# Moving the mLSTM query eviction from VectorE to ScalarE by taking the norm's scale out of it

## The chip, the cores and the metric

The kernel runs on one core of one Trainium2 chip. The metric is the device time of one execution in microseconds (us), the median of several runs. A core has five engines that run side by side, each with its own in-order list of instructions: TensorE (PE, matmuls; its weight loads are shown apart as PEld), VectorE (DVE), ScalarE (ACT), GpSimd (POOL) and SyncE (SP, which here only issues DMAs). They wait for one another by semaphores. Matmul results land in PSUM, from which DVE or ACT has to read ("evict") them before PE may use that buffer again.

## The reference, cut to what matters

Two layers, each on 512 prompt tokens and 8 x 16 sample tokens (640 in all, width 1024): a norm, one wide input projection, three token mixers, an output projection and an MLP. The change is in the mLSTM mixer, which has four heads of 256.

```python
u = rms_norm(x, norm1_g)             # y = x * rsqrt(mean(x*x) + EPS), times g
z = u @ w_in
...
q_m = mq.reshape(B, S, M_HEADS, M_HEAD_DIM)
k_m = mk.reshape(B, S, M_HEADS, M_HEAD_DIM) * (M_HEAD_DIM ** -0.5)
...
# mlstm_chunk
w = einsum('bhtd,bhsd->bhts', q, k) * exp(log_d - m_t[..., None])
num = einsum('bhts,bhsd->bhtd', w, v) + inter_w[..., None] * einsum('bhtd,bhde->bhte', q, C)
den = sum(w, axis=-1) + inter_w * einsum('bhtd,bhd->bht', q, n)
h = num / maximum(abs(den), exp(-m_t))[..., None]
...
h_m = rms_norm(h_m, m_norm_g...)     # per head
```

The kernel multiplies x by the norm's gain alone and projects that, so every projected column still lacks the token's factor rsqrt(mean + EPS), and each eviction multiplies it in. Call the factor r. For the queries it stands in `num` and in `den` alike, so it cancels in `num / maximum(abs(den), exp(-m_t))` as soon as the lower bound `exp(-m_t)` is divided by r too.

## The kernel before

Every large matmul is written as three products of rounded halves (high x high, high x low, low x high), so each weight block is loaded by SP (`wraw`, two buffers), its high half cast by ACT (`whi`, line 164) and its low half made by DVE (`wlo`, line 166). Two forms are used in the stretch of the change: `gemm_w` (line 293, channels on the partitions, 2 tiles of 48 instructions) and `gemm_x` (line 311, tokens on the partitions, 5 tiles of 24 instructions). Both write `acc` buffers in PSUM, of which there are two; an `acc` buffer holds one tile of `gemm_w` or two of `gemm_x`. The latter go through the two buffers by turns: the first half of one, the first half of the other, then their second halves.

Before the layers' mixers, `norm_scale` leaves r in two layouts, `rtok` (a column for each 128 tokens) and `rbc` (along the free dimension, equal on all partitions), and mean + EPS in `vv`.

For each of the four heads of a layer, `mlstm` projects the keys K (`gemm_x`, evicted by ACT at line 621), the queries Q (`gemm_w`, two tiles, evicted by DVE at line 626 into `qT` with a multiplication by `rbc`), the values V (`gemm_x`, ACT, line 633) and an output gate (`gemm_x`, ACT and DVE, lines 616 and 617). From `qT` DVE makes `qs` and `qw` (lines 657 and 658), the queries weighted for the carried state, and ACT and DVE make `qm` (lines 661 and 663) from `qw`. Then come five steps of the recurrence, four on the prompt and one on the samples. A step multiplies kT by qT (line 672), weights the product on DVE (`pt`, line 675), multiplies by V (line 679) and so on. The fifth calls `sample`, which goes through 8 samples: each has its own 256 x 256 state C, loaded by SP into `cb` (five buffers, line 585), cast by ACT into `ch` (line 589) with a rest `cl` on DVE (line 590), multiplied with `qm` on PE (line 593), updated by a product on PE (line 597) and DVE (line 599), and stored by SP (line 601). A load into a `cb` buffer has to wait until the store of what was in it has landed. After `sample` a chain of some twenty small DVE instructions makes the denominators (`fin`, lines 706 to 713); the last DVE step writes `num` (line 715), which PE transposes (line 721) and ACT evicts into `yt` (lines 722 and 725).

The lower bound is `tokq[:, :, 1, h]`, made once for each layer by `mlstm_gates` (line 510, transposed and copied out at lines 529 and 530) and used at line 707.

The order on each engine is not written by hand: a scheduler places the program's instructions engine by engine with a cost model of its own, so a change of a few lines can move everything near it. Its result is that `sample` of head h runs beside K, Q and V of head h + 1, and that of the last head beside the gate projections that follow.

Of the kernel before, what the change touches and what calls it, by code (L numbers as in the profile page):

```python
# [9 lines left out]
F32 = mybir.dt.float32  # L10
# [3 lines left out]
ALU = mybir.AluOpType  # L14
# [61 lines left out]
def trunk(ctx: ExitStack, tc: tile.TileContext, I, O):  # L76
# [3 lines left out]
    pe, act, dve, pool, sp = nc.tensor, nc.scalar, nc.vector, nc.gpsimd, nc.sync  # L80

    const = ctx.enter_context(tc.tile_pool(name="const", bufs=1))
# [32 lines left out]
    def halves(t, n=320):  # L115
        return t.rearrange("p (s t) -> p s t", s=2)
# [238 lines left out]
    rbc = const.tile([128, NT], F32, name="rbc")  # L355
    rtok = const.tile([128, 8], F32, name="rtok")
# [2 lines left out]
    rth = const.tile([128, 8], F32, name="rth")  # L359
    vv = const.tile([128, 8], F32, name="vv")  # L360
    tt = const.tile([128, 8], F32, name="tt")

    def take_x(m, x, g):

        u = act_tile()
        split(u, x, g)
        if m == 0:
            ssum[0] = xp.tile([128, NT], F32, name="ssq", tag="ssq", bufs=1)
        ssq = ssum[0]
        if m == 0:  # L370
            act.activation(ssq, x, AF.Square)
        else:
            sq = tr.tile([128, NT], F32, name="sq", tag="sg")
            act.activation(sq, x, AF.Square)
            dve.tensor_tensor(ssq, ssq, sq, ALU.add)
        return u
# [75 lines left out]
    def mlstm_gates(l, gp, gtp):  # L452
        tokq, decb, m0 = gp
# [74 lines left out]
            pe.transpose(pt, pk[:, 128 * t:128 * t + 128], ident)  # L528
        dve.tensor_copy(tokq[:, 0:4], ps.rearrange("p (t j r) -> p t j r", t=4, j=4)[:, :, :, 0:4])
        dve.tensor_copy(tokq[:, 4], ps2[:, 0:128].rearrange("p (j r) -> p j r", j=4)[:, :, 0:4])  # L530
        sp.dma_start(O["m_p"][l, 0].rearrange("(h o) -> h o", o=1), mrow[:, 511:512])
        sp.dma_start(O["m_s"][l].rearrange("b h -> h b"), mrow[:, 527:640:16])

# [2 lines left out]
    def mlstm(l, gp, gpp, mp, half, hdp):  # L536
        tokq, decb, m0 = gp
# [3 lines left out]
        def wide(nm, shape):  # L541
            return hdp.tile(shape, F32, name=nm, tag="at")
# [67 lines left out]
        for h in range(4):  # L610
            ktok, qT, vt = wide("ktok", [128, 5, 256]), wide("qT", [128, 2, NT]), wide("vt", [128, 5, 258])
# [11 lines left out]
            gemm_x(u, ev_k)  # L623

            def ev_q(m, acc):
                dve.tensor_tensor(halves(qT[:, m, :]), acc[:, :, 0:320], halves(rbc), ALU.mult)  # L626

            gemm_w(u, ev_q)
            pool.memset(vt[:, :, 256:257], 1.0)
            pool.memset(vt[:, :, 257:258], 0.0)  # L630
# [353 lines left out]
    for l in range(depth):  # L984
# [234 lines left out]
        for j in range(1, 4):  # L1219
            branch_a(j)  # L1220
            if j == 1:
                mlstm_gates(l, gp, gtp)
# [242 lines left out]
```

## Time and profile before

| | |
|---|---|
| median of 3 runs | 2901.0 us (2899.3 to 2907.68) |
| the profiled execution | 2899.9 us |
| its span, first to last instruction | 2898.1 us |
| PE busy | 2839.4 us, 98% |
| DVE busy | 1853.8 us, 64% |
| ACT busy | 1312.4 us, 45% |
| mean granted TensorE clock | 0.995 of full speed |

The span is what the trace covers; 1.8 us of the execution lie around it. An engine's busy time is the sum of its instructions' times without the waits. With one engine at 98% the others are read by one question: when do they make that one wait.

### The profile page before, as it was taken

The page shows a single profiled execution, that of the slowest core. Times are in us where ns is not written, and L with a number is a line of the kernel's source. Part 1 is how long each engine was busy: PE and PEld are TensorE (multiplying, and loading weights), DVE is VectorE, ACT ScalarE, POOL GpSimd, SP SyncE. Part 2 cuts the span into 40 slices and gives each one's busy share as a digit, 9 for nine tenths or more (in the row PEclk, how much of TensorE's full clock was granted, in tenths as well). Part 3 has the DMA queues.
Part 4 walks back from the last instruction along what each step waited for, and adds up shares of the span by engine and source line. Part 5 has one row for each costly group of instructions (what it writes and reads, how often), then busy time and mean ns, then how long its engine had stood idle before and what let it go on. Part 6 is the DMA issues. An engine that isn't in the chain of part 4 may idle for free. (4 is left out here: it accounts for less than half of the span.)

```text
span 2898.1 us, 50789 instructions
## 1 busy us (share of the span) xinstructions
PE 2839.4 (98%) x20134; PEld 2799.9 (97%) x20134; DVE 1853.8 (64%) x3758; ACT 1312.4 (45%) x2767; POOL 26.7 (1%) x65
## 2 busy tenths in 40 slices
PE   8999999999999999999999999999999999999999
PEld 8999999999999999999999999999999999999999
DVE  7967566444565677676679676655445646667772
ACT  5764444333442445444357544443444324443452
POOL 0000000000000000000000000000000000000000
PEclk9999999999999999999999999999999999999999
DMA  5242224444573322222322322334445733222222
GB/s 174 65 123 81 76 82 123 120 136 138 158 259 125 104 72 81 81 80 81 113 67 79 116 73 84 96 101 147 131 141 152 264 110 102 74 88 73 80 81 81
DMA packets 276878, 319.53 MB, mean 110 GB/s; under 512 B 26424, under 2 KB 231016, under 8 KB 276608
## 3 DMA queue, kind: packets, MB, share of 16 engines
q1 hardware_dynamic: 267104, 300.03, 33.8%
q10 hardware_dynamic: 9536, 16.26, 1.6%
q8 instruction: 158, 2.59, 0.4%
q14 instruction: 80, 0.66, 0.1%
HBM read 255.76 MB, written 62.04 MB: 110 GB/s over the span
## 5 line engine op out<-in xcount | busy, mean ns | idle before, releaser
L293 PE MATMUL acc<-at,whi 128*128 128x320 f32 x5120 | 818.0, 312 | 6.9 <-ACT at L133 2.8
L293 PEld LDWEIGHTS acc<-at,whi 128*128 128x128 f32 x5120 | 765.3, 189 | 10.2 <-ACT at L133 3.4
L164 ACT CAST whi<-wraw 128x512 fp32r<-128x512 f32 x680 | 406.9, 619 | 512.7 <-PE acc L293 186.9
L166 DVE TENSOR_TENSOR wlo<-wraw,whi 128x512 fp32r<-128x512 f32 x680 | 451.3, 693 | 173.7 <-ACT whi L164 113.5
L311 PE MATMUL acc<-whi,at 128*128 128x256 f32 (+1 forms) x3040 | 408.5, 284 | 16.9 <-DVE qT L626 4.5
L293 PE MATMUL acc<-at,wlo 128*128 128x320 f32 x2560 | 415.6, 310 | 0.0
L311 PEld LDWEIGHTS acc<-whi,at 128*128 128x128 f32 x3040 | 378.2, 188 | 22.1 <-DVE qT L626 5.5
L293 PEld LDWEIGHTS acc<-at,wlo 128*128 128x128 f32 x2560 | 384.1, 188 | 0.7
L255 PE MATMUL acc<-at,whi 128*128 128x320 f32 x1536 | 266.9, 314 | 8.4 <-ACT at L130 5.5
L255 PEld LDWEIGHTS acc<-at,whi 128*128 128x128 f32 x1536 | 236.9, 191 | 14.4 <-ACT at L130 6.1
L311 PE MATMUL acc<-wlo,at 128*128 128x256 f32 (+1 forms) x1520 | 218.6, 282 | 0.2 <-DVE wlo L166 0.2
L311 PEld LDWEIGHTS acc<-wlo,at 128*128 128x128 f32 x1520 | 196.4, 188 | 0.6 <-DVE wlo L166 0.5
L277 PE MATMUL psb<-at,whi 128*128 128x320 f32 x896 | 171.1, 309 | 0.0
L277 PE MATMUL acc<-at,whi 128*128 128x320 f32 x896 | 169.0, 309 | 0.0
L255 PE MATMUL acc<-at,wlo 128*128 128x320 f32 x768 | 143.8, 310 | 0.0
L277 PEld LDWEIGHTS psb<-at,whi 128*128 128x128 f32 x896 | 141.6, 188 | 0.0
L277 PEld LDWEIGHTS acc<-at,whi 128*128 128x128 f32 x896 | 140.9, 188 | 0.0
L164 ACT CAST whi<-wsum 128x512 fp32r<-128x512 f32 x128 | 79.0, 619 | 129.1 <-PE acc L277 93.3
L255 PEld LDWEIGHTS acc<-at,wlo 128*128 128x128 f32 x768 | 121.5, 190 | 0.0
L166 DVE TENSOR_TENSOR wlo<-wsum,whi 128x512 fp32r<-128x512 f32 x128 | 87.8, 689 | 46.9 <-ACT whi L164 45.1
L277 PE MATMUL acc<-at,wlo 128*128 128x320 f32 x448 | 101.8, 308 | 0.0
L277 PE MATMUL psb<-at,wlo 128*128 128x320 f32 x448 | 100.6, 308 | 0.0
(372 smaller groups left out, 3613.1 us busy)
## 6 DMA issues: line engine op xcount, KB each, us to landing
wraw<-in_w_in SPq DMA_DIRECT2D x160, 512.0 KB
wraw<-in_w_up SPq DMA_DIRECT2D x64, 512.0 KB
wraw<-in_w_down SPq DMA_DIRECT2D x64, 512.0 KB
cb<-in_state_mlstm_C SPq DMA_DIRECT2D x64, 256.0 KB
out_C_s<-cb SPq DMA_DIRECT2D x64, 256.0 KB
gdr<-sg ACTq DMA_DIRECT2D x32, 320.0 KB
rl<-ydr SPq DMA_DIRECT2D x32, 320.0 KB
sg<-gdr SPq DMA_DIRECT2D x32, 320.0 KB
```

The lines of the kernel that those rows point to most:

```text
L164: act.copy(hi if shape else hi[:, :, :src.shape[-1]], src)
L166: dve.tensor_tensor(lo if shape else lo[:, :, :src.shape[-1]], src, h.bitcast(F32), ALU.subtract)
L255: pe.matmul(bank[nm], ws[i][:, k, :], xs(nm, k)[:, part], start=(first and i == 0 and k == 0 and part == 0), stop=(i == 1 and k == 3), ski ...
L277: pe.matmul(o[s], lhs, hs[k][:, part, 320 * s:320 * s + 320], start=(k == 0 and i == 0 and part == 0), stop=(i == 1 and k == 3))
L293: pe.matmul(acc[:, s, 0:320], lhs, xs[k][:, part, 320 * s:320 * s + 320], start=(i == 0 and k == 0 and part == 0), stop=(i == 1 and k == 7),)
L311: pe.matmul(o, xs[k][:, part, 128 * t:128 * t + 128], wt[:, k % KQ, 0:n], start=(i == 0 and k == 0 and part == 0), stop=(i == 1 and k == 7),)
```

## The change

The query eviction becomes a plain copy by ACT, so `qT` holds the queries without r. In return `mlstm_gates` multiplies the lower bound by `rinv` = `rtok` x `vv`, which is r / r^2 = 1 / r. All users of `qT` (lines 657, 658 and 672) are linear in it, so `num` and `den` come out divided by r.

```diff
+    rinv = const.tile([128, 8], F32, name="rinv")
...
         dve.tensor_copy(tokq[:, 4], ps2[:, 0:128].rearrange("p (j r) -> p j r", j=4)[:, :, 0:4])
+
+        dve.tensor_tensor(rinv[:, 0:5], rtok[:, 0:5], vv[:, 0:5], ALU.mult)
+        dve.tensor_tensor(tokq[:, :, 1, :], tokq[:, :, 1, :], rinv[:, 0:5].unsqueeze(2).to_broadcast([128, 5, 4]), ALU.mult)
...
             def ev_q(m, acc):
-                dve.tensor_tensor(halves(qT[:, m, :]), acc[:, :, 0:320], halves(rbc), ALU.mult)
+
+                act.copy(halves(qT[:, m, :]), acc[:, :, 0:320])
```

The scheduler then orders the mLSTM stretch of both layers anew; what stands before and after it on PE is as it was but for a handful of places. Line numbers after the change are higher by 4 from `mlstm` on and by 5 behind `ev_q`.

ACT, beside the query projection of head 1, where `sample` of head 0 runs. The names: `ch` is the cast of a sample's state, `nsr` and `csum` small copies of `sample`, `whi` the weight casts, here for V. Before:

```order
L607 COPY csum<-psb 64x258
L602 COPY nsr<-cb 128x2 x2
L589 CAST ch<-cb 128x516 x2
L164 CAST whi<-wraw 128x2x256
L602 COPY nsr<-cb 128x2
L164 CAST whi<-wraw 128x2x256
L589 CAST ch<-cb 128x516
L164 CAST whi<-wraw 128x2x256
L602 COPY nsr<-cb 128x2
L661 CAST qm<-qw 128x8x16
L607 COPY csum<-psb 64x258
L589 CAST ch<-cb 128x516
```

And after:

```order
L611 COPY csum<-psb 64x258
L631 COPY qT<-acc 128x640
L606 COPY nsr<-cb 128x2
L164 CAST whi<-wraw 128x2x256 x3
L606 COPY nsr<-cb 128x2
L593 CAST ch<-cb 128x516 x2
L164 CAST whi<-wraw 128x2x256
L606 COPY nsr<-cb 128x2
L631 COPY qT<-acc 128x640
L593 CAST ch<-cb 128x516
L666 CAST qm<-qw 128x8x16
L611 COPY csum<-psb 64x258
```

The two copies into `qT` stand in ACT's list now, the first behind a `csum` copy, the second behind two casts of states 6 and 7 and a weight cast.

SP at the same place, from the store of head 0's carried prompt state (`out_C_p`) on: `cb` loads of states, `out_C_s` their stores, `kvs` keys and values of a sample's tokens, `dmat` a table of decays, `wraw` a weight block. Before:

```order
L702 DMA out_C_p<-cp 128x2x256
L647 DMA dmat<-adr 128x640
L601 DMA out_C_s<-cb 128x2x256
L585 DMA cb<-in_state_mlstm_C 128x2x256
L577 DMA kvs_5412<-sdr_80 16x2x514 x2
L601 DMA out_C_s<-cb 128x2x256
L577 DMA kvs_5412<-sdr_80 16x2x514
L212 DMA wraw<-in_w_in 128x4x256
L585 DMA cb<-in_state_mlstm_C 128x2x256
L212 DMA wraw<-in_w_in 128x4x256
L601 DMA out_C_s<-cb 128x2x256
```

And after:

```order
L707 DMA out_C_p<-cp 128x2x256
L652 DMA dmat<-adr 128x640
L212 DMA wraw<-in_w_in 128x4x256 x2
L605 DMA out_C_s<-cb 128x2x256
L589 DMA cb<-in_state_mlstm_C 128x2x256
L581 DMA kvs_5415<-sdr_80 16x2x514 x2
L605 DMA out_C_s<-cb 128x2x256
L581 DMA kvs_5415<-sdr_80 16x2x514
L589 DMA cb<-in_state_mlstm_C 128x2x256
L605 DMA out_C_s<-cb 128x2x256
L589 DMA cb<-in_state_mlstm_C 128x2x256
```

The two weight loads stood behind the first two stores, one on each side of a state's load; now they stand ahead of the first store, and stores and loads of states follow one another with no weight load between them until the fourth store. On DVE the eviction (line 626) is simply gone from the list.

PE where `sample` of head 0 begins (the first product of its state 0 with `qm`). Before:

```order
L679 MATMUL psb<-vt,pt 128x257
L593 MATMUL psb<-ch,qm 128x258
L593 MATMUL psb<-cl,qm 128x258
L593 MATMUL psb<-ch,qm 128x258
L593 MATMUL psb<-cl,qm 128x258
L597 MATMUL psb<-kvs_5412 128x258 x2
L593 MATMUL psb<-ch,qm 128x258
L593 MATMUL psb<-cl,qm 128x258
L593 MATMUL psb<-ch,qm 128x258
L593 MATMUL psb<-cl,qm 128x258
L311 MATMUL acc<-whi,at 128x256 x16
L311 MATMUL acc<-wlo,at 128x256 x3
```

And after:

```order
L684 MATMUL psb<-vt,pt 128x257
L597 MATMUL psb<-ch,qm 128x258
L597 MATMUL psb<-cl,qm 128x258
L597 MATMUL psb<-ch,qm 128x258
L597 MATMUL psb<-cl,qm 128x258
L601 MATMUL psb<-kvs_5415 128x258 x2
L597 MATMUL psb<-ch,qm 128x258
L597 MATMUL psb<-cl,qm 128x258
L597 MATMUL psb<-ch,qm 128x258
L597 MATMUL psb<-cl,qm 128x258
L293 MATMUL acc<-at,whi 128x320 x19
L597 MATMUL psb<-ch,qm 128x258
```

Before, the rest of K stands between the beginning of `sample` and the query projection (line 293); after, the query projection follows at once. After the change this is so for heads 0, 1 and 2 of both layers, whose lists on PE are nearly alike from there to the transposes of `num` (250, 250 and 251 matmuls); before, the three differ, and in the third the query projection is already half a tile old when `sample` begins.

## Rows read from the trace of the kernel before

**Rows 1.** The page: span, and busy time of PE with its share.

```profile
span 2898.1 us, 50789 instructions
PE 2839.4 (98%) x20134; PEld 2799.9 (97%) x20134; DVE 1853.8 (64%) x3758; ACT 1312.4 (45%) x2767; POOL 26.7 (1%) x65
```

**Rows 2.** Windows, mLSTM of both layers: stretch, length, busy PE PEld DVE ACT POOL, clock, DMA.

```profile
480.00:766.00 286.00, 276.28 (x2118) 269.28 (x2117) 148.58 (x411) 117.79 (x290) 0.28 (x4) 1.00 0.49 142
1924.00:2207.00 283.00, 275.29 (x2112) 268.76 (x2111) 147.07 (x408) 117.09 (x289) 0.28 (x4) 1.00 0.48 143
```

**Rows 3.** Waits of PE, whole span: who waited for whom, total us, times, longest.

```profile
PE acc L311 <- DVE qT L626: 4.5, 4, 1.4
PE psb L593 <- ACT ch L589: 4.0, 5, 1.2
PE acc L311 <- ACT vt L633: 3.4, 7, 0.6
...
PE psb L721 <- DVE num L715: 3.0, 3, 1.2
```

**Rows 4.** Windows, from a sample's first L593 to its first L721: heads 0-2, both layers.

```profile
548.27:588.53 40.26, 36.47 (x272) 35.19 (x271) 26.71 (x77) 15.37 (x40) 0.14 (x2) 1.00 0.58 176
631.53:670.60 39.07, 35.52 (x265) 34.22 (x263) 25.96 (x76) 15.86 (x41) 0.14 (x2) 1.00 0.61 178
716.20:751.50 35.30, 32.91 (x251) 31.97 (x249) 23.55 (x72) 15.65 (x41) 0.00 (x0) 1.00 0.66 198
1990.32:2029.92 39.60, 36.69 (x272) 35.30 (x271) 26.72 (x78) 15.16 (x40) 0.14 (x2) 1.00 0.61 182
2072.90:2110.71 37.81, 35.17 (x264) 34.32 (x263) 26.04 (x76) 15.24 (x40) 0.14 (x2) 1.00 0.63 182
2156.29:2191.10 34.81, 32.65 (x251) 31.93 (x249) 23.62 (x72) 15.75 (x41) 0.00 (x0) 1.00 0.60 181
```

**Rows 5.** Groups by shape: line, engine, tile, shape, count | busy us, mean ns | idle before.

```profile
L626 DVE TENSOR_TENSOR qT<-acc,rbc 128x640 f32<-128x640 f32 x16 | 13.1, 820 | 0.6 <-PE acc L293 0.6
L707 DVE TENSOR_TENSOR fin<-fin,tokq 128x5 f32<-128x5 f32 x8 | 1.3, 168 | 0.1
L1343 ACT COPY s<-acc 128x320 f32<-128x320 f32 x96 | 40.7, 424 | 34.8 <-PE acc L255 34.1 <-DVE ha L1355 0.6
L1286 ACT ACTIVATE ha<-x,cv 128x640 f32<-128x640 f32 x16 | 13.3, 830 | 35.3 <-DVE x L1282 35.3
L642 ACT COPY kT<-psb 128x512 f32<-128x512 f32 x16 | 9.7, 606 | 0.0
```

**Rows 6.** Timeline of PE, layer 0: start, length, instructions [idle before, releaser].

```profile
479.80 2.04 PE L311 MATMUL acc<-whi,at 128*128 128x256 f32 x16
481.68 1.11 PE L311 MATMUL acc<-wlo,at 128*128 128x256 f32 x8
...
574.06 0.46 PE L293 MATMUL acc<-at,wlo 128*128 128x320 f32 x2
...
579.47 2.15 PE L311 MATMUL acc<-whi,at 128*128 128x256 f32 x16 [1.38 <-DVE qT L626]
```

**Rows 7.** Timeline of DVE just before that wait of PE ends.

```profile
578.20 0.48 DVE L599 SCALAR_TENSOR_TENSOR cb<-cb,decb,psb 128x258 f32<-128x258 f32 x1
578.59 0.82 DVE L626 TENSOR_TENSOR qT<-acc,rbc 128x640 f32<-128x640 f32 x1
```

**Rows 8.** Timeline of ACT, layer 0, `sample` of head 2.

```profile
738.58 0.62 ACT L589 CAST ch<-cb 128x516 fp32r<-128x516 f32 x1 [4.30 <-DMA cb<-in_state_mlstm_C]
739.23 0.47 ACT L633 ACTIVATE vt<-acc,rtok 128x256 f32<-128x256 f32 x1
```

**Rows 9.** Timeline of PE, same stretch: the waits of that `sample`.

```profile
734.33 0.39 PE L593 MATMUL psb<-ch,qm 128*128 128x258 f32 x1 [0.53 <-ACT ch L589]
739.76 1.45 PE L311 MATMUL acc<-whi,at 128*128 128x256 f32 x10 [0.60 <-ACT vt L633]
751.50 0.33 PE L721 MATMUL psb<-cs,num 128*128 128x128 f32 x1 [1.24 <-DVE num L715]
```

## The prediction

> **What bounds the kernel now.** I began with the page's busy times: PE works for 2839.4 of 2898.1 us [rows 1], so the change can only take away some of PE's 58.7 us of idling, add to it, or leave it; PE's own work is not touched. Next the windows of the two stretches in which mLSTM runs: PE is idle for 286.00 - 276.28 = 9.72 us in the first layer and 283.00 - 275.29 = 7.71 us in the second, 17.43 us in all, at a granted clock of 1.00; DVE is busy for 148.58 of 286.00, 52%, and ACT for 117.79, 41% [rows 2]. So no engine but PE is near its limit there, and the whole stake of the change is 17.4 us, 0.6% of the time.
>
> Where in the stretch these 17.4 us lie: I cut out of each layer the three parts that run from the first product of a `sample` with `qm` to the first transpose of `num`. PE's idle time in them is 3.79, 3.55, 2.39, 2.91, 2.64 and 2.16 us, 17.44 in sum [rows 4]. That is all of it: outside these six parts mLSTM has no waits of PE. The list of PE's waits gives the causes: query evictions 4.5 us in 4 waits, `ch` casts 4.0 in 5, `vt` evictions 3.4 in 7, `num` 3.0 in 3 [rows 3]; that is 14.9, and the other 2.5 us are small ones.
>
> **The change part by part.** *Removed:* sixteen query evictions on DVE of 820 ns [rows 5], 13.1 us, all of them beside PE's work except where PE waits for them (the 4.5 us). *Added:* sixteen copies of 128x640 from PSUM on ACT. The trace has no such copy of that size. Two ACT copies give a slope: 606 ns for 512 columns and 424 for 320 [rows 5], 182 / 192 = 0.95 ns a column, so 606 + 128 x 0.95 = 727 ns; an activation of 640 columns took 830 [rows 5]. So the price is between 0.73 and 0.83 us, 11.6 to 13.3 us in all; I take the lower, whose rows are copies of the same kind. ACT goes from 41% to 43% busy. An eviction becomes shorter by 0.1 us or not at all: what counts is when it starts.
>
> *When the copy can start.* In the wait that I looked at, PE ended the second query tile at about 574.5 (its last products ran from 574.06 for 0.46 us [rows 6]); DVE got to the eviction at 578.59, 4.1 us later, behind work of `sample` such as the state update at 578.20 [rows 7]; V's next products needed the buffer, and PE waited 1.38 us [rows 6]. After the change PE has behind the second query tile first one whole V tile that goes into the other buffer: 24 products of 1.88 / 16 = 0.1175 us [rows 6] make 2.8 us, and some nine products of `sample` between them, of about that length, 1.1 more. So the copy has some 3.9 us to start and end before PE wants its buffer. It takes 0.73, with two casts of states 6 and 7 ahead of it, which rows like it price at 0.62 each [rows 8]: 0.73 + 2 x 0.62 = 2.0 us if their states are there. It fits, and the 4.5 us of query waits go. If the states are late, it doesn't; that is rival A.
>
> *The two small instructions* on `rinv` and `tokq`, once a layer, work on 5 and 20 columns; the nearest row is 168 ns for 5 columns [rows 5]. Four of them cost 0.7 us. They run in `mlstm_gates` beside head 0's query projection, where no wait of PE is left over from above (all lie in the six parts). Nothing reads the lower bound before the first denominators, tens of us later. I put them at 0; uncovered they would cost 0.7 us. The trace can't make them a gain, since nothing leaves that place.
>
> *The new order.* It does more than the edit. In the six parts PE's list now takes one form, close to that which the third head had before: the query projection starts at once with `sample`, and 250 matmuls lie there where before there were 272 and 265 in the first two heads and 251 in the third [rows 4]. SP's list changes with it: the two weight loads stand ahead of the first store of a state instead of between the first ones. What ends such a part, once the query waits are gone, is the chain of `sample` itself: a state's store, the next load into its buffer, its cast, its product, and at the end the denominators and `num`, for which PE waited 1.24 us in the third head [rows 9]. The third heads, which had the form, idled for 2.39 and 2.16 us [rows 4], 2.28 in the mean. Six parts at 2.28 give 13.7 us in place of 17.4, a gain of 3.8. That is less than the 4.5 of the query waits, since part of it is given back at `num`. I take this sum, because it is measured on whole parts of that form, waits of every kind included.
>
> The fourth heads' `sample` runs beside the gate projections and has no wait of PE before; I leave it at 0. A wait there would look like those of the other heads, 2.28 us each at most, 4.6 for two layers; it is inside the range.
>
> *Sum:* the profiled execution took 2899.9 us, 2898.1 of span and 1.8 around it. 2899.9 - 3.8 = 2896.1. The median of the runs, 2901.0, is 1.1 above that execution, and so I forecast 2897 us.
>
> **The rivals.** *A, the copies queue behind late states.* On ACT the V evictions and the second query copy stand behind `ch` casts, and a cast waits for its state's load, which waits for a store, on a queue on which two weight blocks now stand first. In the third head of the first layer a cast waited 4.30 us for its load, the V eviction behind it ran only then [rows 8], and PE waited 0.60 us for that [rows 9]. Before, a late state on ACT could hold V only, since Q was DVE's; now it holds Q as well. If such a cast stands ahead of the second copy in each part, the copy starts 4.30 us late; its cover has 3.9 - 2.0 = 1.9 us to spare, so PE waits 4.30 - 1.9 = 2.4 us. At the other end I let only 0.60 us of it be hidden, as much as PE paid in that row: 3.7. Mean 3.05; six parts make 18.3 us on top of the forecast: about 2915 (2911 to 2919). For it: the row itself, and the weight loads ahead of the store. Against it: in that row PE paid only 0.60 of the 4.30. The kernel becomes measurably slower from (8.7 + 3.8) / 6 = 2.1 us a part.
>
> By the Trainium skill, PSUM — Partial Sum Buffer, section Engine vs sequencer instructions, the queues of ScalarE and VectorE are strictly first in, first out, so that an eviction can't pass a waiting cast; the trace agrees [rows 8], where the V eviction began only as the cast ended, at 739.23.
>
> *B, nothing is late next.* If the state chain is not late in the new form (weight loads out of the way of the stores, state loads earlier), what remains are the V evictions: 3.4 us in 7 waits [rows 3], 0.49 each, six of them 2.9 us. Gain 17.4 - 2.9 = 14.5 us, 2886.5. For it: five of the waits named are for `ch` [rows 3], and the casts get their states on another schedule now. Against it: the third heads, in nearly this form, waited for `num` too.
>
> *C, no change.* The query waits of 4.5 us are spent again, one for one, at the next late step: PE arrives earlier and waits longer at `num`. Then 2901. For it: `num` hangs on the state chain, which the change doesn't shorten; a DVE at 52% gains little from 13 us less. Against it: the four query waits fell in the middle of V's tiles, and the state products behind them started later by as much.
>
> The Trainium skill, Perfetto Trace Analysis, section Optimizing Scalar/DVE Operations, says that offloading work to ScalarE may make sense if VectorE is saturated. DVE isn't here [rows 2], and by that rule the time would be that of C. What speaks against it is that PE waits for DVE all the same [rows 3].
>
> *It doesn't do what it says:* if the copy takes 0.83 rather than 0.73, an eviction is no shorter than on DVE, 0.82. That alone moves nothing, as the start decides.
>
> **How the numbers follow.** Chances: forecast 0.40 (2897), B 0.22 (2886.5), C 0.20 (2901), A 0.18 (2915). About 0.3%, 8.7 us, is what a measurement of this kernel can tell from no change: faster means under 2892.3, slower over 2909.7. The forecast and C lie within it, B below, A above from its lower end on. With a little of the forecast's tail on the fast side, faster has 0.25, slower 0.19, and 0.56 is left for no change. The range: PE can't gain more than the 17.4 us, 2883.6, so B's case lies between there and 2890, and 2885 leaves out little of it (0.04); on the other side 2912 takes in the uncovered 0.7 of the small instructions, the 4.6 of the fourth heads on top of C (2906) and A's lower end, and leaves out 0.16 of A. So 2885 to 2912.
>
> **What the profile after would show.** *Right:* PE's waits no longer name `qT`; the six parts idle for about 2.3 us each, `num` the largest cause; PE's busy time the same within a few us; ACT's copies into `qT` at 0.73 us. *A:* waits of PE for `qT` on ACT, with casts ahead of them that waited for `cb` loads, and parts that idle for 4 us and more. *B:* parts that idle for half a us, and no wait for `num`. *C:* the query waits gone and those for `num` longer by as much. *Wrong in the reading:* if the gain or loss lies outside the six parts, in a stretch whose order barely changed, or if PE's busy time or granted clock moves by more than the waits; then the sum, which takes both as given, fails at its first step.

## The result, and the profile after

The changed kernel takes 2918.9 us (median of 6 runs, 2915.5 to 2921.7) against 2900.4 for the kernel before beside it; the ratio is 1.0052 (95% interval 1.0041 to 1.0064). It is slower, by 0.5%. The forecast was 2897, the range ended at 2912.

The page of the changed kernel, the line that answers to [rows 1]:

```profile
span 2915.5 us, 50830 instructions
PE 2849.0 (98%) x20134; PEld 2809.2 (96%) x20134; DVE 1842.9 (63%) x3746; ACT 1325.4 (45%) x2783; POOL 26.7 (1%) x65
```

The span grew by 17.4 us. PE has the same 20134 instructions and is busy for 9.6 us more (2849.0 against 2839.4); it is idle for 66.5 us instead of 58.7, 7.8 more. So there are two losses, and the prediction had allowed for one kind only.

**The idle time.** The list of PE's waits over the whole span (who waited for whom: total us, times, longest), to be held against [rows 3]:

```profile
PE acc L311 <- ACT vt L638: 17.2, 6, 3.2
...
PE psb L601 <- DVE cb L603: 2.1, 3, 1.0
...
PE psb L597 <- ACT ch L593: 1.4, 3, 0.6
```

The waits for `qT` (4.5 us) are gone, as are those for `num` (3.0), and those for `ch` fell from 4.0 to 1.4. But PE now waits for the V evictions, six times, 2.9 us each: once in each of heads 1 to 3 of both layers (heads counted from 0; `sample` of head 2 runs beside V of head 3, and is what the prediction calls the third head). Before, that sum was 3.4 us, with 0.6 the longest. The six parts of [rows 4] read now (stretch, length, busy PE PEld DVE ACT POOL, granted clock, DMA):

```profile
552.05:590.26 38.21, 33.90 (x252) 32.77 (x251) 24.11 (x74) 15.33 (x39) 0.14 (x2) 1.00 0.61 182
633.07:672.16 39.09, 35.49 (x252) 34.33 (x251) 25.14 (x76) 15.32 (x39) 0.14 (x2) 0.96 0.58 183
714.96:754.05 39.09, 35.26 (x253) 34.53 (x252) 25.22 (x76) 15.45 (x39) 0.00 (x0) 0.96 0.60 184
2001.89:2043.05 41.16, 36.55 (x253) 35.57 (x252) 25.24 (x76) 15.47 (x39) 0.14 (x2) 0.92 0.57 174
2085.84:2124.95 39.11, 36.17 (x252) 35.65 (x251) 25.24 (x76) 15.54 (x39) 0.14 (x2) 0.91 0.64 187
2167.78:2205.05 37.27, 34.24 (x253) 33.00 (x252) 24.32 (x75) 15.46 (x39) 0.00 (x0) 1.00 0.62 184
```

Idle are 4.31, 3.60, 3.83, 4.61, 2.94 and 3.03 us, 22.3 in all, where it was 17.4 and I had forecast 13.7. The matmuls in the six parts are now the same (252 or 253 recorded), as the order had said.

**The clock.** The seventh figure shows the second loss: four of the six parts have a mean granted clock of 0.91 to 0.96; before, all six had 1.00. PE's timeline at the fourth V tile of head 1, once in each layer, and the windows around the second of these waits:

```profile
586.14 2.17 PE L311 MATMUL acc<-whi,at 128*128 128x256 f32 x16 [2.90 <-ACT vt L638]
...
2036.18 3.78 PE L311 MATMUL acc<-whi,at 128*128 128x256 f32 x16 [2.91 <-ACT vt L638]
```

```profile
2030.00:2036.00 6.00, 3.26 (x28) 3.06 (x26) 3.67 (x16) 1.77 (x6) 0.00 (x0) 0.96 0.56 185
2036.00:2042.00 6.00, 5.82 (x27) 5.82 (x28) 3.86 (x18) 0.57 (x3) 0.00 (x0) 0.50 0.55 188
2042.00:2048.00 6.00, 6.00 (x52) 6.00 (x52) 2.63 (x5) 5.50 (x12) 0.00 (x0) 0.97 0.22 37
```

After the wait of 2.91 us the clock stood at 0.50, its lower level of 1.2 GHz, for these 6 us; 27 matmuls ran where 52 run in the next 6, and 16 of them took 3.78 us instead of the 2.17 after the wait of the first layer, which was as long but left the clock at 1.00. Taken us by us, the clock was 0.50 from 667 to 670, 749 to 752, 2036 to 2042 and 2118 to 2124. So a wait of this size cost itself, and in four of six cases half of what PE would have done in the next 3 to 7 us.

**Why the eviction is late.** PE goes through V's tiles in the order 0, 2, 1, 4, 3; tile 4 takes the buffer of tiles 0 and 1, so it needs the eviction of tile 1 as soon as tile 1 is made. I follow the wait of 2.90 us back. The timeline of ACT, just ahead of it:

```profile
582.73 0.62 ACT L593 CAST ch<-cb 128x516 fp32r<-128x516 f32 x1 [1.88 <-DMA cb<-in_state_mlstm_C]
584.59 0.19 ACT L606 COPY nsr<-cb 128x2 f32<-128x2 f32 x1 [1.23 <-DVE cb L603]
585.51 0.19 ACT L606 COPY nsr<-cb 128x2 f32<-128x2 f32 x1 [0.74 <-DVE cb L603]
585.61 0.83 ACT L638 ACTIVATE vt<-acc,rtok 128x256 f32<-128x256 f32 x2
```

The eviction (585.61) stands behind two two-column copies `nsr` of states 6 and 7 of head 0, which wait for their update on DVE, and behind the cast of state 1 of head 1, which waits for its load. DVE over the same time:

```profile
581.08 0.19 DVE L713 RECIPROCAL fin<-fin 128x5 f32<-128x5 f32 x1
583.39 0.69 DVE L594 TENSOR_TENSOR cl<-cb,ch 128x516 fp32r<-128x516 f32 x1 [2.12 <-ACT ch L593]
584.00 0.15 DVE L714 TENSOR_TENSOR fin<-ss,fin 128x5 f32<-128x5 f32 x1
584.08 0.87 DVE L603 SCALAR_TENSOR_TENSOR cb<-cb,decb,psb 128x258 f32<-128x258 f32 x2
...
585.01 0.47 DVE L603 SCALAR_TENSOR_TENSOR cb<-cb,decb,psb 128x258 f32<-128x258 f32 x1
```

Three of the four updates of states 6 and 7 (line 603) and the denominators (`fin`) stand behind `cl`, the rest of state 1 of the *next* head, which for 2.12 us waits for that same cast. And SP shows why the cast is late:

```profile
573.73 0.39 SPq L589 DMA_DIRECT2D cb<-in_state_mlstm_C  x1
574.93 0.40 SPq L605 DMA_DIRECT2D out_C_s<-cb  x1
575.53 1.58 SPq L212 DMA_DIRECT2D wraw<-in_w_in  x2
577.51 0.37 SPq L589 DMA_DIRECT2D cb<-in_state_mlstm_C  x1
```

The load of state 1 was issued at 577.51, behind two weight blocks; its cast began at 582.73, 5.2 us later. That of state 0, issued at 573.73 without them, was cast after 2.7 us (576.42). The work on state 1 isn't needed before the next `sample`, some 50 us later. ACT's list and DVE's both have it in front of work that is needed now.

### The profile page after: what moved, and what is told of

Its sections match the earlier page's. It is cut to its first block, busy times and chain, and to the rows that moved or that the text cites. A ratio compares the mean times of both kernels' runs of the same rounds, so it can differ in the third digit from the quotient of the medians.

```text
span 2915.5 us, 50830 instructions
## 1 busy us (share of the span) xinstructions
PE 2849.0 (98%) x20134; PEld 2809.2 (96%) x20134; DVE 1842.9 (63%) x3746; ACT 1325.4 (45%) x2783; POOL 26.7 (1%) x65
## 5 line engine op out<-in xcount | busy, mean ns | idle before, releaser
L311 PE MATMUL acc<-whi,at 128*128 128x256 f32 (+1 forms) x3040 | 415.1, 287 | 27.4 <-ACT vt L638 17.2
L311 PEld LDWEIGHTS acc<-whi,at 128*128 128x128 f32 x3040 | 385.0, 192 | 32.0 <-ACT vt L638 18.5
```

Source lines behind the costliest of these rows:

```text
L311: pe.matmul(o, xs[k][:, part, 128 * t:128 * t + 128], wt[:, k % KQ, 0:n], start=(i == 0 and k == 0 and part == 0), stop=(i == 1 and k == 7),)
```

## The experiments

An edge `behind(a, b)` in the diffs lets the scheduler place `a` only behind `b` in the list of their engine; it adds no semaphore. `vev[1]` is the V eviction of tile 1 of the same head. Ratios are to the kernel before on the same chip, with 95% intervals. The waits are those of the one profiled execution of each run; that of e4_wlate took 2900.2 us, the shortest of its ten.

In the expectations, theory O is the order on ACT, theory D the order on ACT and DVE together, S the swap itself, and M the chain of stores and loads of the states whatever the order.

| run | edit | us | ratio | PE waits for vt / num, us |
|---|---|---|---|---|
| after | | 2918.9 | 1.0052 (1.0041 to 1.0064) | 17.2 / 0 |
| e1_pin | after, cast of state 1 behind V | 2908.9 | 1.0036 (1.0023 to 1.0049) | 12.7 / 3.1 |
| e2_dve | after, query copy on DVE | 2898.8 | 0.9999 (0.9989 to 1.0008) | 3.4 / 3.3 |
| e3_rev | before, one ACT pair swapped | 2900.6 | 1.0004 (0.9994 to 1.0013) | 6.1 / 0 |
| e4_wlate | after, weights behind store 6 | 2905.7 | 1.0022 (1.0012 to 1.0032) | 3.9 / 0.3 |
| e5_nsr | after, two nsr on GpSimd | 2910.4 | 1.0040 (1.0025 to 1.0055) | 3.8 / 11.7 |
| e6_nsr_pin | e5 and e1 | 2909.4 | 1.0032 (1.0021 to 1.0044) | 2.7 / 14.1 |
| e7_before_nsr | before, two nsr on GpSimd | 2899.8 | 1.0001 (0.9992 to 1.0010) | 4.5 / 3.4 |
| e8_nsr_all | after, all nsr on GpSimd | 2910.2 | 1.0039 (1.0025 to 1.0054) | 4.2 / 12.2 |
| e9_fin | after, DVE: denominators first | 2898.7 | 0.9998 (0.9989 to 1.0008) | 4.5 / 2.5 |
| e10_fin_nsr | e9 and e5 | 2900.2 | 1.0004 (0.9994 to 1.0013) | 4.3 / 2.7 |
| e11_before_fin | before, DVE: denominators first | 2893.9 | 0.9983 (0.9974 to 0.9993) | 3.6 / 0 |
| e12_wlate_nsr | e5, weights behind store 4 | 2896.0 | 0.9992 (0.9983 to 1.0002) | 6.5 / 1.6 |
| e13_rows_only | after, DVE: only n rows moved | 2913.3 | 1.0046 (1.0031 to 1.0060) | 15.9 / 0 |
| e14_all_mended | e9, e5, weights behind store 4 | 2892.5 | 0.9974 (0.9964 to 0.9983) | 6.3 / 0 |
| e15_before_both | e11, weights behind store 4 | 2896.6 | 0.9989 (0.9980 to 0.9998) | 6.6 / 0 |

### Is it the swap, or the order?

**e2_dve** keeps everything of the change but the engine.

```diff
-                act.copy(halves(qT[:, m, :]), acc[:, :, 0:320])
+                dve.tensor_copy(halves(qT[:, m, :]), acc[:, :, 0:320])
```

> The changed kernel with the query eviction as a plain copy on DVE instead of ACT (the lower bound is still multiplied by rinv). The order of PE, ACT, SP and POOL is then that of the kernel before, instruction by instruction, and DVE has four small instructions more. Theory O: like before, 2896 to 2904 us, PE's waits for qT on DVE are there again (4 to 5 us), those for vt about 3.4, no clock dip in the mLSTM stretches. Rival S in its other half (the raw queries or the rinv instructions cost something): over 2908.

It came out as the kernel before, 0.9999, with these waits of PE:

```profile
PE acc L311 <- DVE qT L631: 4.4, 4, 1.3
...
PE acc L311 <- ACT vt L638: 3.4, 5, 1.4
```

The order on PE, ACT and SP is that of the kernel before. One thing came out otherwise than expected: a single wait for `num` of 3.11 us in the first layer was followed by a granted clock of 0.52 from 752.70 to 756.20; I had expected no fall. Raw queries and the small instructions on `rinv` cost nothing that can be measured. What costs is what the move to ACT brings with it.

**e3_rev** takes nothing of the change and swaps one pair of neighbours on ACT in head 3, in each layer:

```diff
                 ins = act.copy(nsr[:, b, h, :], cb[:, :, 256])
+                if b == 7:
+                    lastn[0] = ins
...
                 iv = act.activation(vt[:, t, 0:256], o, AF.Copy, scale=rtok[:, t:t + 1])
+                if t == 1 and h > 0:
+                    behind(iv, lastn[0])
```

> The kernel before (DVE eviction, nothing of the change) with one edge of order added: the V eviction of tile 1 stands on ACT behind the small copy nsr of state 7 of the head before. In each layer this swaps exactly one pair of neighbouring ACT instructions, in head 3, and leaves every other row of every engine where it was. In the kernel before that eviction ran 1.8 us ahead of this copy. Theory O: the order alone makes PE wait for vt at the fifth tile of head 3, by about 1.3 to 2.0 us in each layer, where it did not wait before; with no or little loss of clock the kernel gets 2 to 6 us slower (2902 to 2907). Rival S: no ACT copy is added, so nothing changes: 2898 to 2902.

```profile
746.46 2.15 PE L311 MATMUL acc<-whi,at 128*128 128x256 f32 x16 [1.86 <-ACT vt L640]
```

The wait came in the first layer, 1.86 us where there had been none; in the second, where 0.47 had been, it was 0.48, since state 7 was done in time. The time did not move beyond its interval (1.0004), and lies where rival S had it: the wait for `num` behind it in the first layer, 1.24 us in [rows 9], was gone. So order alone makes such a wait, in one place of two; what it cost was paid out of a later one, which I had not put in. That order costs time is not shown by this run; e9_fin, below, shows it.

### Freeing the V eviction on ACT

**e1_pin** moves the cast of state 1 behind the eviction, **e5_nsr** takes the two `nsr` copies off ACT (PE, DVE and SP keep their lists row for row), **e6_nsr_pin** does both.

```diff
                 ich = act.copy(ch, cb)
+                if b == 1:
+                    behind(ich, vev[1])
```

> The changed kernel with one edge of order added: the cast ch of a sample's state 1 stands on ACT behind the second V eviction of its head (no wait is added or taken away). Theory O (order on ACT: the second V eviction of heads 1 to 3 stands behind the cast of state 1, whose load is late, and PE waits 2.4 to 3.2 us for it six times; the granted clock then falls for some us): PE's waits for vt fall from 17.2 us to about 3 to 5 (0.5 to 0.8 each), no clock below 0.98 in the mLSTM stretches, so 17.2 - 4 = 13 us of waits and most of the 9.6 us that PE was busier come back: about 2895 us (2890 to 2901). Rival S (the swap itself: ACT with sixteen copies more is too slow for V): waits for vt stay over 12 us, 2913 or more. Rival L (the late state load is what costs; freeing V only moves the wait to the products of state 1 or to num): waits for vt fall, but those for ch, cl or num rise by 10 us or more: 2905 to 2915.

The waits for `vt` fell only to 12.7 us, 2.1 each. With the cast out of the way `cl` went behind the updates too, and yet `nsr` of state 7 waited for its update, and that, on DVE, behind an n row (`cb<-nT`, the copy of a state's n vector into its `cb` buffer) that waited for a store:

```profile
583.95 0.17 DVE L594 COPY cb<-nT 128x4 f32<-128x4 f32 x1 [1.50 <-DMA out_C_s<-cb]
...
584.61 0.19 ACT L612 COPY nsr<-cb 128x2 f32<-128x2 f32 x1 [2.40 <-DVE cb L609]
```

```diff
-                act.copy(nsr[:, b, h, :], cb[:, :, 256])
+                if b in (6, 7):
+                    pool.tensor_copy(nsr[:, b, h, :], cb[:, :, 256])
+                else:
+                    act.copy(nsr[:, b, h, :], cb[:, :, 256])
```

> The changed kernel with the two-column copies nsr of states 6 and 7 made by GpSimd instead of ACT. PE, DVE and SP keep their rows and their order one for one; on ACT only the two nsr copies ahead of the second V eviction are gone, while the cast of state 1 still stands ahead of it. Theory O, sharpened after the first four runs (the eviction stands behind nsr of state 7, which waits for a state update on DVE, which itself stands behind a copy into a cb buffer that waits for a store, or behind the rest of state 1): the eviction runs right behind the cast, at about 0.5 us after its tile's end; PE's waits for vt fall from 17.2 us to 3 to 6 (six of 0.5 to 1.0), the clock stays at 1.00 in the mLSTM stretches, and 11 to 14 us of waits and 7 to 10 us of PE's busy time come back: 2893 to 2899 us. Rival C (the cast of state 1 and its load are enough to hold the eviction): waits for vt stay over 10 us, 2908 or more. Rival S (ACT too busy through the sixteen copies): the same, over 2908.

Here the waits for `vt` fell as expected, to 3.8 us, and yet 2910 us were left. The waits of PE in e5_nsr, and DVE's timeline with the denominators of head 0:

```profile
PE psb L729 <- DVE num L723: 11.7, 6, 3.2
...
PE acc L311 <- ACT vt L641: 3.8, 6, 0.9
```

```profile
580.03 0.19 DVE L716 RECIPROCAL fin<-fin 128x5 f32<-128x5 f32 x1
582.33 0.70 DVE L594 TENSOR_TENSOR cl<-cb,ch 128x516 fp32r<-128x516 f32 x1 [2.11 <-ACT ch L593]
582.95 0.16 DVE L717 TENSOR_TENSOR fin<-ss,fin 128x5 f32<-128x5 f32 x1
...
586.61 0.17 DVE L590 COPY cb<-nT 128x4 f32<-128x4 f32 x1 [1.03 <-DMA out_C_s<-cb]
...
588.23 2.07 DVE L723 SCALAR_TENSOR_TENSOR num<-num,fin,mo 128x256 f32<-128x256 f32 x5
```

Of 13.4 us freed at `vt`, 11.7 come back at `num`: the chain of the denominators stands behind the same `cl`, which waits 2.11 us here as it did in the changed kernel, and behind the n rows. The place where ACT was blocked was a second result of one cause.

> Both edits together: nsr of states 6 and 7 on GpSimd, and the cast of state 1 pinned behind the second V eviction. Theory O: no wait is left that stands ahead of the eviction, vt waits of 0.45 to 0.6 each (3 to 4 us), 2891 to 2899 us; if the cast now comes too late for state 1, PE waits for ch or cl with 0.5 to 1 us more a head, and it is no better than with the nsr edit alone. Rival C: 2891 to 2899 as well, but clearly better (8 us or more) than with the nsr edit alone.

With both edits the waits for `vt` are down to 0.45 us each, and those for `num` at 14.1. 2909, where 2891 to 2899 was expected: what is left of the loss is not on ACT's list.

> The kernel before (query eviction on DVE) with nsr of states 6 and 7 on GpSimd; only ACT's and GpSimd's lists change, by those rows. It shows what that edit is worth without the change. Theory O: little, since the V evictions there waited for 0.45 to 0.6 us only: 2896 to 2901 us, qT waits of 4 to 5 us remain. If it gains as much as in the changed kernel (over 12 us), what was found isn't an interaction with the change.

> The changed kernel with the nsr copies of all eight states on GpSimd. ACT then has none of the small copies that wait for state updates on DVE ahead of its casts and evictions. Theory O: vt waits of 0.5 to 1.0 as with states 6 and 7 alone, and the casts and the second query copy come a little earlier: 2889 to 2898 us. It isn't meant to tell theories apart but to see whether the swap, once its cost is gone, beats the kernel before (2899).

The `nsr` edit is worth nothing in the kernel before (1.0001), and with all eight copies on GpSimd the changed kernel is as with two (2910.2, where 2889 to 2898 was expected).

### Putting the denominators first on DVE

**e9_fin** leaves ACT and SP row for row as the change has them (and PE's matmuls, compared row by row in the two traces, but for 28 of 20134 places), and places on DVE `cl` of the next head's state 1 and the n rows of states 2 to 4 behind the denominators (`done[0]` is the last of their small instructions in the head before).

```diff
                 icp = dve.tensor_copy(cb[:, :, 256:258], nT[:, :, 8 * b + 2 * h:8 * b + 2 * h + 2])
...
                 icl = dve.tensor_tensor(cl, cb, ch.bitcast(F32), ALU.subtract)
+                if h > 0 and b in (2, 3, 4):
+                    behind(icp, done[0])
+                if h > 0 and b in (1,):
+                    behind(icl, done[0])
...
-            dve.tensor_tensor(r, r, y, ALU.mult)
+            done[0] = dve.tensor_tensor(r, r, y, ALU.mult)
```

> The changed kernel with edges of order on DVE alone: the rest cl of the next head's state 1 and the copies of n rows into the buffers of its states 2 to 4 (each waits for a load or a store) stand behind the small instructions of the denominators instead of among them (two of the n-row copies still stand ahead of the writing of num). ACT and SP keep their rows one for one; nsr of states 6 and 7 and the cast of state 1 still stand ahead of the second V eviction. Theory D (two lists are blocked by the same thing, the next head's early states: on ACT the V eviction behind nsr, on DVE the last state updates and the denominators behind cl and the n rows): the last updates no longer wait for cl, nsr comes at once, PE's waits for vt fall from 17.2 us to 4 to 7; num comes 2 us earlier, with waits for num of 3 to 8 us in all: 2896 to 2905 us. Rival M (the chain of stores and loads of the states has to end first, whatever the order on DVE): waits for vt and num together stay over 13 us: 2906 or more.

2898.7 us, 0.9998: the whole loss is undone. The waits of PE, and the timelines of ACT and DVE at the same eviction as above:

```profile
PE acc L311 <- ACT vt L647: 4.5, 6, 1.3
...
PE psb L735 <- DVE num L729: 2.5, 2, 1.7
```

```profile
582.07 0.62 ACT L598 CAST ch<-cb 128x516 fp32r<-128x516 f32 x1 [1.89 <-DMA cb<-in_state_mlstm_C]
582.60 0.28 ACT L615 COPY nsr<-cb 128x2 f32<-128x2 f32 x2
582.79 0.83 ACT L647 ACTIVATE vt<-acc,rtok 128x256 f32<-128x256 f32 x2
```

```profile
581.71 0.48 DVE L612 SCALAR_TENSOR_TENSOR cb<-cb,decb,psb 128x258 f32<-128x258 f32 x1
...
584.38 0.70 DVE L599 TENSOR_TENSOR cl<-cb,ch 128x516 fp32r<-128x516 f32 x1
```

The cast still waits 1.89 us for its load and still stands ahead of the eviction. But the last update (581.71) is done before it, `cl` comes behind, the `nsr` copies no longer wait, and the eviction starts 0.72 us after the start of the cast instead of 2.88. The six parts idle for 1.63, 1.85, 2.08, 1.48, 2.77 and 1.32 us, 11.1 in all, and all have a granted clock of 1.00; PE is busy for 2840.7 us, 1.3 more than before instead of 9.6. First and fifth part:

```profile
551.94:587.55 35.61, 33.98 (x254) 32.89 (x253) 23.62 (x72) 15.26 (x39) 0.14 (x2) 1.00 0.60 185
...
2069.18:2106.08 36.90, 34.13 (x253) 32.95 (x251) 23.57 (x72) 16.03 (x40) 0.14 (x2) 1.00 0.58 181
```

**e10_fin_nsr** adds the `nsr` edit, **e11_before_fin** puts the same edges on DVE of the kernel before, **e13_rows_only** moves the n rows alone.

> The same edges on DVE, and nsr of states 6 and 7 on GpSimd besides. Compared with the run with the nsr edit alone (2910, waits for num 11.7 us, for vt 3.8) only DVE's order differs, and a little of PE's. Theory D: waits for num fall to 3 to 8 us, vt as before 3 to 5: 2895 to 2904 us. Rival M: waits for num stay at 10 to 13 us and the time at 2907 to 2912.

Against e5_nsr ACT and SP have the same rows; the waits for `num` fall from 11.7 to 2.7 us and the time from 2910 to 2900.

> The changed kernel with only the copies of n rows (states 2 to 4 of the next head) behind the denominators on DVE; the rest cl of state 1 stays among them, ahead of the last state updates. ACT and SP keep their rows. If cl is the block (theory D's main part: it waits about 2 us for its cast, and behind it stand the updates on which nsr and so the second V eviction wait): waits for vt stay at 10 to 17 us, 2906 to 2916. If the n rows are the block: waits for vt fall to 4 to 7 us, 2896 to 2903.

2913.3, with 15.9 us of waits for `vt`: moving the n rows alone does next to nothing for these waits, since `cl` still stands ahead of the updates. In e1_pin it was the other way round: `cl` had gone behind them and an n row held them. So either is enough to block, and both have to go. (An edge for `cl` alone was not run.)

> The kernel before (query eviction on DVE) with the same edges on DVE. It shows what they are worth without the change. Theory D: the waits for num (3.0 us) fall under 1.5, those for qT (4.5), ch (4.0) and vt (3.4) stay about as they are: 2894 to 2900 us. If it comes out clearly under the changed kernel with the same edges, the swap costs something even where its new order is mended.

2893.9, 0.9983: the same edges gain in the kernel before too. The waits for `num` are gone; but those for `qT` fell as well, from 4.5 to 1.0 us, which I had not expected. Here the scheduler moved more than DVE's rows: compared in the same way, PE's matmuls differ from those of the kernel before in some 1200 places, so the gain is that of a new order and not of the edges alone.

### The loads behind it

**e4_wlate** and **e12_wlate_nsr** move the two weight blocks of a head's gate projection on SP behind a later store of a state (6 or 4; `late` holds their places in the list of weight jobs, `stx` that store). The second also has the `nsr` edit.

```diff
             wlast[0] = sp.dma_start(raw[:, :, :n], ap[512 * hf:512 * hf + 512, :].rearrange("(k p) c -> p k c", p=128))
+            if j in late and stx[0] is not None:
+                behind(wlast[0], stx[0])
```

> The changed kernel with one edge of order added on SP: the two weight blocks of a head's gate projection are loaded behind the store of state 6 of the head before, so that they no longer stand ahead of the loads of the next states 0 and 1. On ACT the cast of state 1 and two nsr copies still stand ahead of the second V eviction. Theory O with a late load: state 1 lands 2 us or more earlier, and the waits for vt fall to 3 to 7 us in all, no or one clock dip: 2893 to 2905 us, if the weight blocks come early enough for the gate projection; if they don't, PE waits for whi there, up to 2 us a head. Rival S: the waits for vt stay over 12 us. If the load's place on SP is not what makes state 1 late, the waits stay as well, with the casts still waiting for cb loads.

> The changed kernel with nsr of states 6 and 7 on GpSimd, and the two weight blocks of a head's gate projection loaded behind the store of state 4 (not 6, as in the earlier run) of the head before. Theory D says the loads are one cause of the lateness and the lists behind them the other: with the blocks out of the way the states come earlier, so that waits for vt are 3 to 5 us, for num 0 to 5, and the blocks come early enough that waits for mo stay under 6 (12.8 with state 6): 2892 to 2902 us. If waits for mo stay over 10 us, 2902 or more. Rival M predicts a gain here too, so this run tells D from M only together with the others: by D order and loads can each be mended, by M only the loads.

With the blocks later, e4_wlate casts state 1 of head 1 2.8 us after the issue of its load, instead of 5.2:

```profile
574.58 0.37 SPq L597 DMA_DIRECT2D cb<-in_state_mlstm_C  x1
...
577.34 0.62 ACT L601 CAST ch<-cb 128x516 fp32r<-128x516 f32 x1 [2.49 <-DMA cb<-in_state_mlstm_C]
```

The waits for `vt` went to 3.9 us. ACT's list changed with it, other than the expectation says: of the two `nsr` copies only that of state 6 stayed ahead of the second V eviction. The blocks then came too late: PE waited 12.8 us for `mo`, the gate's evictions, 3.6 the longest. Behind store 4 (e12_wlate_nsr) that is gone and the time is 2896, though the waits for `vt` were 6.5 us, over the 3 to 5 expected. These edges rearrange a good deal of the order, so they show that the late loads are one link of the chain, not how much each row is worth.

**e14_all_mended** and **e15_before_both** put the edits together, with the query eviction on ACT and on DVE.

> The changed kernel with the three edits that helped: DVE's denominators first, nsr of states 6 and 7 on GpSimd, the two weight blocks behind the store of state 4. If they add up, the six parts idle under 8 us in all and the time is 2888 to 2895 us, under the kernel before (2898) and about where the kernel before with the DVE edges is (2894). If the DVE edges and the later weights free the same wait, no more than the better of the two: 2894 to 2900.

> The kernel before (query eviction on DVE) with DVE's denominators first and the two weight blocks behind the store of state 4. It asks whether the swap is worth anything once the lists are mended: if it comes out under the run with all mended on the changed kernel by 3 us or more, the swap is not wanted; if above it by as much, it is. By the run with the DVE edges alone (2894) I expect 2888 to 2896 us.

e14_all_mended is faster than both kernels: 2892.5 us, 0.9974 (0.9964 to 0.9983). The two evictions compare one way under the DVE edges alone (2898.7 with ACT, 2893.9 with DVE) and the other way with the weights moved too (2892.5, which has the `nsr` edit besides, against 2896.6). By the rule of the last expectation the swap would be wanted, as e15_before_both came out 4.2 us above; but each is an order of its own, so no worth of the swap by itself, of either sign, is shown; in these two pairs it is within some 5 us.

## Why the prediction was wrong

**What bounds the kernel: right.** Nearly all that changed lies in the six parts and in what follows their waits. (That mLSTM has no other waits of PE holds from 480 and 1924 on, where the windows of [rows 2] begin; just ahead of them PE waits 1.72 us a layer for `ktok`, the eviction of K, before and after alike.) Outside them PE's idle time rose by 2.9 us (from 41.3 to 44.2), most of it two single waits (for `rtok`, 1.7 to 2.7, which e11_before_fin shows too, and one of 1.5 for `mo`).

**PE's own work is not touched: wrong.** The sum had a term for idle time and none for the clock. PE was busy for 9.6 us more with the same instructions, over half of the loss, and more than its idle time grew; the prediction had named this as a sign that its sum fails at the first step. That the clock belongs to the six waits is shown by e9_fin, where the waits are short, no part is under 1.00, and 8.3 of the 9.6 us are gone.

**The copies: right.** The group of the copy in the profile of the changed kernel:

```profile
L631 ACT COPY qT<-acc 128x640 f32<-128x640 f32 x16 | 11.0, 687 | 3.5 <-PE acc L293 3.4
```

687 ns against the 727 forecast from the slope, under both ends of the range. They fit into their cover, and the 4.5 us of query waits went. But they fit more narrowly than reckoned, and partly by luck. ACT and PE around the second copy of head 1:

```profile
574.94 0.19 ACT L606 COPY nsr<-cb 128x2 f32<-128x2 f32 x1 [2.88 <-DVE cb L603]
575.04 0.69 ACT L631 COPY qT<-acc 128x640 f32<-128x640 f32 x1
```

```profile
570.36 0.61 PE L293 MATMUL acc<-at,wlo 128*128 128x320 f32 x3
...
576.96 1.34 PE L311 MATMUL acc<-whi,at 128*128 128x256 f32 x10
```

Directly ahead of the copy stood not a cast but an `nsr` (the lists under "The change" show it), which waited for a state update. The copy ended 4.8 us after its tile, where 2.0 was reckoned and 3.9 was the cover; PE came back to the buffer only after 6.0, since it had waits of its own on the way. In the other five parts the copy ended 3.3 to 4.0 us after its tile. The small instructions cost nothing: e2_dve.

**The new order idles like the third head before, 2.28 us a part: this is the step that failed.** Measured are 22.3 / 6 = 3.7 us. I had taken the third head's form from PE's list alone, and SP's as the one other list that changed. In the third head before, DVE did the update of state 6 and the first six instructions of the denominators ahead of the `cl` of the next head's state 1, ACT had two V evictions ahead of that state's cast, not one, and tile 1's eviction stood ahead of `nsr` of state 7 (the pair that e3_rev swaps). DVE in the kernel before, the last update ahead of that `cl`, and the `cl`:

```profile
743.96 0.47 DVE L599 SCALAR_TENSOR_TENSOR cb<-cb,decb,psb 128x258 f32<-128x258 f32 x1
745.51 0.70 DVE L590 TENSOR_TENSOR cl<-cb,ch 128x516 fp32r<-128x516 f32 x1 [1.07 <-ACT ch L589]
```

In the new order both engines have the early states of the next head in front. The lists of DVE and ACT were there to read as well; a part of the program has the form of another only if all its lists have. With DVE's list mended, e9_fin, the six parts idle for 11.1 us and the kernel takes 2898.7: near the 13.7 and the 2897 that I had forecast. The forecast was that of a kernel with another order on DVE; that e9_fin comes so near it is no proof of the sum, since its list on DVE is not the third head's either.

**Rival A: right in kind, and it had 0.18.** An eviction on ACT behind late states, 2.4 to 3.7 us a part on top of the forecast's, about 2915, 2911 to 2919: the waits were 2.4 to 3.2 us and the time 2918.9. Three things differ. It was V's second eviction, not the query copy, that was caught; I had looked at what stands ahead of the copies and not at what they push behind. The late cast reached it by way of DVE (`cl`, the updates, `nsr`), as e9_fin shows. And the waits themselves replaced others, so that idle time grew by 7.8 us only, the clock making up the rest; the price came out right by luck, by two errors that cancel. The rule from the Trainium skill that stood beside it (PSUM — Partial Sum Buffer, Engine vs sequencer instructions: strict first in, first out) is borne out on both engines by the rows at 583.39 and 585.61.

**Rival B and C: no.** The waits for `vt` were not 0.49 each. C's mechanism, a gain given back at `num`, did not occur in the changed kernel, where `num` made no wait at all; it occurred in e5_nsr, where 11.7 of 13.4 us freed at `vt` came back there. The Trainium skill, Perfetto Trace Analysis, section Optimizing Scalar/DVE Operations, names a saturated DVE as the case in which an offload to ScalarE may make sense. DVE was busy for 52% of the stretch [rows 2], and no worth of the swap by itself is shown, in keeping with it; but the loss came from the order, of which that rule does not speak.

## What to carry to other kernels

Where a scheduler places the instructions, an edit that moves one operation is a new order on every engine; compare all lists of the stretch, and for each instruction that waits ask whether what is queued behind it is needed sooner than itself. Work for a later stage that waits for a load (here the early states of the next head) is worth trying behind the end of the present stage on every in-order list; edges of order can say that. Here it paid on DVE (e9_fin); on ACT alone (e1_pin, e6_nsr_pin) it left 10 us. When a wait is freed and the time stays, look for the next wait on the same cause before calling the first reading wrong: e5_nsr freed an eviction and PE waited for `num`, with one `cl` ahead of both.

## What the runs showed of the hardware

The granted clock of TensorE fell to its lower level after four of six waits of 2.4 to 3.2 us, and stayed there for 3 to 7 us while PE was busy again; after two waits of 2.90 and 2.40 us it did not fall. In e9_fin, where no wait of PE in the mLSTM stretches was over 1.72 us, it fell nowhere there. No length that is safe follows from that: in e8_nsr_all the mean clock was 0.62 from 668.00 to 672.50, behind a wait of 1.80 us, and in e11_before_fin 0.72 from 2174.00 to 2180.00, around one of 1.88. In the changed kernel one such wait cost up to about twice its own length.

A load of 256 KB was cast 5.2 us after its issue when two blocks of 512 KB had been issued just ahead of it on the same queue, and 2.7 us after it without them; with the blocks moved away (e4_wlate) the load of the same state was cast after 2.8.
